# x and the first weights in eight shared transfers, compressed scores from whole queries, TensorE's steps in a new order

## The chip, the cores and the metric

One Trainium2 chip, one core. The engines are TensorE (PE, with its weight loads PEld), VectorE (DVE), ScalarE (ACT), GpSimd (POOL) and SyncE (SP), which only issues transfers here. The metric is the device time of one execution in microseconds, the median of several; the kernel before has 271.18 (three runs, 270.7 to 273.65).

## What is computed

Two decoder layers over x of 256 positions by 1024 channels, float32. The even layer has one input projection that feeds two groups of heads, NSA (8 heads; compressed blocks, selected blocks and a window, with gates) and MoBA (8 heads), each with its own gating path; the odd layer is gated linear attention (GLA, 4 heads). Each layer ends in a LayerNorm.

```python
def even_layer(x, w_in, ..., w_out, ln_g, ln_b):
    h = x @ w_in
    nq, nkv, ngate, nz, mq, mk, mv, mz = _split(h, EVEN_SPLITS)
    ...
    y = jnp.concatenate([o_nsa * jax.nn.silu(nz), o_moba * jax.nn.silu(mz)], axis=-1) @ w_out
    return layer_norm(DEEPNORM_ALPHA * x + y, ln_g, ln_b)

def odd_layer(x, w_in, gate_w2, gate_b, gn_g, w_out, ln_g, ln_b):
    h = x @ w_in
    q, k, v, g_lr, z = _split(h, ODD_SPLITS)
    log_a = jax.nn.log_sigmoid((g_lr @ gate_w2 + gate_b).astype(f32)) / GLA_TAU
    o = gla_mix(q, k, v, log_a)
    ...
    y = (o * jax.nn.silu(z)) @ w_out
    return layer_norm(DEEPNORM_ALPHA * x + y, ln_g, ln_b)
```

The compressed branch of NSA scores each query against 15 compressed keys; these scores are what the step s computes.

## The kernel before

**Products.** A dense product is done with both operands split in two: hi is the operand rounded to TensorE's 32-bit format (a cast), lo the rest (a subtraction). Each product is three matmuls, hi by hi, hi by lo, lo by hi. The contraction over 1024 channels is eight blocks of 128; `denseB` gives a result of 128 columns of the weights by 256 positions (24 matmuls), `denseA` one of 128 positions by up to 512 columns (24 matmuls).

**Weights.** They come in units of 1024 to 1120 columns of 128 partitions, in the order of the steps. `load_unit` issues the unit's transfer on SP into one of six raw buffers (`wr`); a transfer waits until the unit six earlier has been split. `split_unit` casts hi on ACT and subtracts lo on DVE or POOL, as the string `LO_ON` says by unit (V or G), into one of eight slots. `prepare_for` keeps the splits about two units ahead of the step that uses them.

**The head.** The first two units (K and V columns that the compressed branch needs, called "first") come in four halves of 256 KB on SP, x transposed (xT) in four pieces of 256 KB on ACT's queue. Each of four rounds casts one weight half and one xT piece on ACT and makes the low halves on DVE; TensorE does 12 matmuls a round into two PSUM banks (48 in all, one line in the profile, L324). Seven idle matmuls run before. Then Q0.0 and Q0.1, the first queries, are two `denseB` steps of their own on the next two units.

**The order.** TensorE's and SP's orders are the order in which the code is written, given by the step strings `EVEN` and `ODD`. Q, C, V, k, q, v, z, e, o with a number are dense steps; w, h, g, s, t, u are the compressed branch of NSA; Nja to Nje the scores, transposes and outputs of the NSA head group j (a and b scores, c, d transposes of the exponentials, e outputs), Mja, Mjc, Mje those of MoBA; in the odd layer n and N are LayerNorm, T the transposes of its rows, G and g the gate, I and L the levels of GLA, X its diagonals, A its outputs, U the gated rows. ACT, DVE and POOL run in an order fixed by a scheduler when the kernel is built; each engine does its instructions strictly in that order, so a late one holds what stands behind it. `AT_ODD` says behind which step a small load (gate weights, masks, LayerNorm weights) is issued.

**Attention steps.** For a head, DVE computes masked scores and their maxima, ACT the exponentials, and then the rows are scaled by 1/sum (times the gate for NSA) on the engine that `SC_ON` names for that step (A, V or G). TensorE transposes the scaled rows into one of two t banks, ACT copies them to SBUF (PT), and the outputs follow. PSUM has three d banks, two s, two t and one o.

**Names used.** hilo is a split unit, raw an unsplit one, pr the exponentials, PT their transposes, xt the split x, gl the transposed gate input, gw the gate's weights (gwh, gwl its halves), zg the gated rows. The function `cmp_s` is the step s: per head group t it multiplies the compressed keys kcf with the hi and then with the lo part of the queries, 4 matmuls each.

Of the kernel before, what the change touches and what calls it, by code (L numbers as in the profile page):

```python
# [7 lines left out]
F32 = mybir.dt.float32  # L8
# [7 lines left out]
P = 128  # L16
# [11 lines left out]
EVEN = """Q0.0 Q0.1 C0.0 V0.0 N0a C0.1 V0.1 w Q1.0 N0b h v0.0 N1a g Q1.1 v0.1 s N0c N1b N0d t k0.0 N1c k0.1 N2a u q0.0  # L28
N2b N1d N0e M0a q0.1 N2c N1e N2d M1a M0c k1.0 N3a N2e N3b M1c k1.1 q1.0 q1.1 z0.0 M0e M2a N3c z1.0 N3d M3a
M1e z0.1 M2c N3e M3c z2.0 z2.1 M2e z1.1 M3e z3.0 z3.1"""  # L30
# [4 lines left out]
ODD = """e0.0 e1.0 e0.1 n0 T0 e1.1 v1.0 v3.0 v0.0 n1 T1 v3.1 v0.1 G k0.1 g k0.0 q0.0 q0.1 q1.1 k1.1 I0 L1:0 k1.0 q1.0  # L35
L2:0 L4:0 v1.1 L8:0 I1 v2.0 L1:1 z0.0 z0.0+ L2:1 L4:1 z0.1 L8:1 z0.1+ L16:1 L16:0 z1.0 L32 z1.1 z1.0+ L64
v2.1 X L128 A0 z1.1+ U0 A1 o0.0 U1 o1.0 N0 o1.1 o0.1 N1"""
AT_EVEN = {"Q0.1": "w1", "N1c": "ln ev", "z3.0": "x"}
AT_ODD = {"k0.1": "gate", "e0.0": "masks", "q1.1": "ln od"}

LO_ON = "VVVVGGVVVVVGVVVVVGVVVVGVVVGVGVVVGGGGVVVVVGVVVGVGVGVVVVVVVVVVVVVVVVGVGVVV"

CP_ON = "AAVV"

SC_ON = "AVAGAGAVVVGV"
MK_BUFS = 2
# [67 lines left out]
def build(tc, I, out):  # L114
# [12 lines left out]
    with ExitStack() as ctx:  # L127
# [32 lines left out]
        def load_unit():  # L160
            k, n = SHAPES[len(raws)]
            raw = wr.tile([P, UMAX], F32, tag="raw", name=nm("raw"))
            rv = raw[:, :k * n].rearrange("p (k n) -> p k n", k=k)
            src = I["w"][at[0]:at[0] + P * k * n].rearrange("(p k n) -> p k n", p=P, k=k)
            at[0] += P * k * n
            for ks in ((slice(0, 2), slice(2, 4)) if len(raws) < 2 else (slice(0, k),)):
                nc.sync.dma_start(rv[:, ks], src[:, ks])
            raws.append(rv)

        def split_unit():  # L170
            u = len(units)
            k, n = SHAPES[u]
            t = wx.tile([P, 2, UMAX], F32R, tag="hilo", name=nm("hilo"))
            hv = t[:, :, :k * n].rearrange("p a (k n) -> p a k n", k=k)
            units.append(hv)
            if u < 2:
                return
            A.copy(hv[:, 0], raws[u])  # L178
            ENG[LO_ON[u]].tensor_sub(hv[:, 1], raws[u], hv[:, 0].bitcast(F32))  # L179

# [62 lines left out]

        xq = [cp.tile([P, 4, S], F32, tag=f"x{h}", name=nm("xT")) for h in range(2)]
        load_unit()
        for q in range(4):
            A.dma_start(xq[q // 2][:, 2 * (q % 2):2 * (q % 2) + 2], I["xT"][:, 2 * q:2 * q + 2])
        load_unit()
# [56 lines left out]

        xt = new_xt()
        fill[0] = 7
        pks = [bank("d"), bank("d")]
        prepare(2)
        for q in range(4):  # L310
            xs = xq[q // 2][:, 2 * (q % 2):2 * (q % 2) + 2]
            ks = slice(2 * q, 2 * q + 2)
            hv, rv = units[q // 2], raws[q // 2]
            us = slice(2 * (q % 2), 2 * (q % 2) + 2)
            A.copy(hv[:, 0, us], rv[:, us])
            A.copy(xt[:, 0, ks], xs)  # L316
            V.tensor_sub(hv[:, 1, us], rv[:, us], hv[:, 0, us].bitcast(F32))
            V.tensor_sub(xt[:, 1, ks], xs, xt[:, 0, ks].bitcast(F32))
            for n in range(3):
                for k in range(2 * q, 2 * q + 2):  # L320
                    for i in range(2):
                        wh, wl = (t[:, i * P:(i + 1) * P] for t in tile_of("first", k))
                        a, b = ((wh, xt[:, 0, k]), (wl, xt[:, 0, k]), (wh, xt[:, 1, k]))[n]
                        T.matmul(pks[i][:, :S], a, b, start=(k == n == 0), stop=(k == KC - 1 and n == 2))  # L324
        prepare(4)
# [17 lines left out]
        for i, pd in enumerate(pks):  # L343
            split_psum(KH[:, i], KL[:, i], pd[:, :S])
# [21 lines left out]
        def queries(j, i):  # L366
            pd = bank("d")
            denseB(pd[:, :S], f"even Q{j}", i, xt)
            q = [ep.tile([P, S], F32R, name=f"Q{n}{2 * j + i}") for n in "hl"]
            split_psum(*q, pd[:, :S])  # L370
            Q.append(q)
# [638 lines left out]
def layout(inputs):  # L1010
# [45 lines left out]
```

## Time and profile before

| | |
|---|---|
| median of three runs | 271.18 us |
| lowest, highest | 270.7, 273.65 us |
| the profiled execution, by its own time | 271.48 us |
| its span in the profile | 269.7 us |
| TensorE busy | 258.1 us, 96% |
| DVE, ACT, POOL busy | 188.7, 163.7, 69.4 us |
| TensorE's dense steps, L221 and L202 | 112.1 and 90.2 us busy |

The rows that follow are of one profiled execution. Times count from the start of its span. An engine is busy while it has an instruction under way; matmuls are pipelined, so the spans of neighbouring ones overlap. "Idle before" in square brackets is what the engine stood still just before a group, with what released it.

### The profile page before, as it was taken

To read this page: it belongs to the slowest core of one execution; us is meant where nothing else is said; L and a number is where in the kernel's file an instruction comes from. 1 tells how busy PE (TensorE), PEld (TensorE's weight loads), DVE (VectorE), ACT (ScalarE), POOL (GpSimd) and SP (SyncE) were. 2 spreads that over 40 slices of the span, in tenths; PEclk is the share of its full clock that TensorE was granted. 3 is DMA by queue.
4 is the path that set the end of the run, shared out by engine and by line. 5 is a ranking of instruction groups with operands and counts; after the bars stand their busy time and mean duration, and the time that the engine had idled before them with its cause. 6 is when DMAs were issued, how large, how long until landed. Compare 5 with 4: busy or idle time off the path is not lost.

```text
span 269.7 us, 5534 instructions
## 1 busy us (share of the span) xinstructions
PE 258.1 (96%) x2111; PEld 226.6 (84%) x2111; DVE 188.7 (70%) x411; ACT 163.7 (61%) x383; POOL 69.4 (26%) x58
## 2 busy tenths in 40 slices
PE   5999999999999999999999999999999999899990
PEld 2999987879887999899888899899997779688880
DVE  2888699796675575648839994657793793675745
ACT  4776658879887857845407526696973746853000
POOL 1070030823500344039402350807000003510101
PEclk9999999999999999999999999999999999999997
DMA  6999968754431062005950664775374260000012
GB/s 201 416 378 407 408 228 251 266 193 198 156 91 70 2 202 113 0 2 187 370 237 21 220 233 169 239 306 179 139 239 154 84 229 2 1 2 0 12 66 78
DMA packets 15035, 45.50 MB, mean 169 GB/s; under 512 B 2673, under 2 KB 3825, under 8 KB 15009
## 3 DMA queue, kind: packets, MB, share of 16 engines
q1 hardware_dynamic: 13856, 43.59, 45.4%
q10 hardware_dynamic: 1152, 1.57, 1.8%
q8 instruction: 16, 0.26, 0.4%
q14 instruction: 11, 0.08, 0.1%
HBM read 44.10 MB, written 1.05 MB: 167 GB/s over the span
## 4 chain that ended last, share of the span: by engine, by line
PE 80%; DVE 9%; DMA 3%; issue 3%; ACT 2%; POOL 1%; DVEq 0%; SPq 0%; ACTq 0%; POOLq 0%
PE d L202 31%; PE d L221 29%; PE s L338 3%; PE d L324 3%; DVE hilo L179 3%; PE t L549 2%; DVE x L288 2%; DMA gw<-gw 2%; ACT hilo L178 1%; DMA raw<-w 1%; PE o L569 1%; PE o L612 1%; PE t L603 1%; DVE x L290 1%; DVE lnst L276 1%
## 5 line engine op out<-in xcount | busy, mean ns | idle before, releaser
L221 PE MATMUL d<-hilo,xt 128*128 128x512 f32 (+3 forms) x600 | 112.1, 344 | 0.2 <-DVE xt L154 0.2
L221 PEld LDWEIGHTS d<-hilo,xt 128*128 128x128 f32 x600 | 93.4, 188 | 14.1 <-DVE xt L154 0.4
L202 PE MATMUL d<-xt,hilo 128*128 128x256 f32 x720 | 90.2, 284 | 0.0
L202 PEld LDWEIGHTS d<-xt,hilo 128*128 128x128 f32 x720 | 86.9, 189 | 1.3 <-issue 1.1
L178 ACT CAST hilo<-raw 128x1024 fp32r<-128x1024 f32 (+2 forms) x68 | 71.0, 1053 | 18.6 <-PE d L221 13.9
L179 DVE TENSOR_TENSOR hilo<-raw,hilo 128x1024 fp32r<-128x1024 f32 (+2 forms) x51 | 70.6, 1391 | 14.5 <-ACT hilo L178 14.3
L179 POOL TENSOR_TENSOR hilo<-raw,hilo 128x1024 fp32r<-128x1024 f32 (+1 forms) x17 | 44.5, 2627 | 125.5 <-ACT hilo L178 113.1
L496 ACT ACTIVATE pr<-ng,sm 128x256 f32<-128x256 f32 (+1 forms) x48 | 21.3, 445 | 7.7 <-DVE sm L495 7.7
L502 POOL TENSOR_SCALAR pr<-pr,sm 128x256 f32<-128x256 f32 (+1 forms) x12 | 11.8, 1000 | 19.3 <-DVE sm L532 13.4
L495 DVE CUSTOM_DVE_ANT_0 ng<-s,b 128x256 f32<-128x256 f32 (+1 forms) x48 | 14.2, 351 | 1.4 <-PE s L338 1.2
L275 DVE SCALAR_TENSOR_TENSOR x<-x,d 128x512 f32<-128x512 f32 (+1 forms) x9 | 5.6, 626 | 12.8 <-PE d L221 12.5
L256 POOL TENSOR_TENSOR lnrs<-lnrs,nhalf 128x1 f32<-128x1 f32 x4 | 2.9, 731 | 33.3 <-DVE lnrs L255 33.3
L324 PEld LDWEIGHTS d<-xt,hilo 128*128 128x128 f32 x48 | 7.7, 249 | 2.4 <-ACT xt L316 2.4
L324 PE MATMUL d<-xt,hilo 128*128 128x256 f32 x48 | 7.9, 339 | 1.5 <-ACT xt L316 1.5
L496 ACT ACTIVATION_READ_ACCUMULATOR pr<-ng,sm 128x1 f32 x48 | 9.0, 188 | 0.0
L636 DVE TENSOR_TENSOR xt<-g,xt 128x256 fp32r<-128x256 f32 x8 | 6.7, 833 | 2.8 <-ACT xt L635 2.8
L288 DVE SCALAR_TENSOR_TENSOR x<-x,lnmv,lng 128x256 f32<-128x256 f32 x16 | 8.5, 592 | 0.0
L976 ACT ACTIVATE xt<-t,gnh 128x128 fp32r<-128x128 f32 x16 | 4.3, 383 | 6.1 <-PE t L973 6.1
L635 ACT CAST xt<-g 128x256 fp32r<-128x256 f32 x8 | 3.3, 407 | 7.8 <-DVE g L634 7.6
L552 ACT COPY PT<-t 128x512 f32<-128x512 f32 (+1 forms) x16 | 7.2, 474 | 1.0 <-PE t L549 0.9
L502 DVE TENSOR_SCALAR pr<-pr,sm 128x256 f32<-128x256 f32 (+1 forms) x20 | 7.5, 435 | 0.2
L795 POOL TENSOR_TENSOR TT<-TT 128x512 f32<-128x512 f32 (+5 forms) x6 | 5.0, 827 | 8.9 <-ACT TT L792 8.5
(191 smaller groups left out, 269.6 us busy)
## 6 DMA issues: line engine op xcount, KB each, us to landing
raw<-w SPq DMA_DIRECT2D x58, 512.0 KB, 4.7
raw<-w SPq DMA_DIRECT2D x8, 520.0 KB, 7.0
w<-w SPq DMA_DIRECT2D x4, 512.0 KB, 8.2
raw<-w SPq DMA_DIRECT2D x2, 560.0 KB, 7.2
xT<-xT ACTq DMA_DIRECT2D x4, 256.0 KB, 6.1
raw<-w SPq DMA_DIRECT2D x4, 256.0 KB, 5.6
x<-x SPq DMA_DIRECT2D x2, 512.0 KB, 3.7
b<-b SPq DMA_DIRECT2D x1, 512.0 KB, 7.5
```

Source lines behind the costliest of these rows:

```text
L178: A.copy(hv[:, 0], raws[u])
L179: ENG[LO_ON[u]].tensor_sub(hv[:, 1], raws[u], hv[:, 0].bitcast(F32))
L202: T.matmul(o, a, b, start=(j == 0), stop=(j == len(terms) - 1))
L221: T.matmul(o, a, b, start=(ks[0] == j == 0), stop=(ks[-1] == KC - 1 and j == len(terms) - 1))
L288: V.scalar_tensor_tensor(x[:, sl], x[:, sl], mv[:, 0:1], g[:, sl], ALU.subtract, ALU.mult)
L324: T.matmul(pks[i][:, :S], a, b, start=(k == n == 0), stop=(k == KC - 1 and n == 2))
L338: T.matmul(o, a[halves[g]], b[halves[g]], start=(n == 0), stop=(n == len(terms) - 1))
L495: V.tensor_tensor_reduce(ng[:, :w], pS, b8[:, h, S - w:], -0.125, 3e38, ALU.add, ALU.min, sm[:, 0:1])
L496: A.activation(pr, ng[:, :w], AF.Exp, bias=sm[:, 0:1], scale=-1.0, accum_out=sm[:, 1:2])
L502: ENG[e].tensor_scalar(pr, pr, coef, None, ALU.mult)
L552: A.copy(dst, pt[:, :2 * P * (c + 1)].rearrange("p (a q) -> p a q", q=P))
L636: V.tensor_sub(mx[:, 1, k], g2, mx[:, 0, k].bitcast(F32))
```

## The change

Three edits.

1. **The head.** The two units of "first" and the two of Q0 are no longer units of the weight stream. Block k of xT (256 columns) and block k of both sets of weights (512 columns) come together in one transfer of 128 by 768 (393 KB), eight in all, on SP, into the six raw buffers, so block 6 and block 7 wait until blocks 0 and 1 have been split. The 96 matmuls (those of "first" and of Q0) run block by block into four banks (two d, two s). The cast of xT is on DVE for the first two blocks, on ACT for the rest. Q0 has no separate matmuls; its queries and KH, KL are split at the end of the head.
2. **s from whole queries.** ACT also copies each query tile whole (128 by 256), and `cmp_s` multiplies kcf with these, 4 matmuls instead of 8.
3. **Orders and engines.** The strings EVEN, ODD, AT_ODD, `LO_ON` (20 splits on POOL instead of 17), `CP_ON` and `SC_ON` (which engine scales each step's rows) are new.

The diff, cut to its core:

```diff
-EVEN = """Q0.0 Q0.1 C0.0 V0.0 N0a C0.1 V0.1 w Q1.0 N0b h v0.0 N1a g Q1.1 v0.1 s N0c N1b N0d t k0.0 N1c k0.1 N2a u q0.0
-N2b N1d N0e M0a q0.1 N2c N1e N2d M1a M0c k1.0 N3a N2e N3b M1c k1.1 q1.0 q1.1 z0.0 M0e M2a N3c z1.0 N3d M3a
-M1e z0.1 M2c N3e M3c z2.0 z2.1 M2e z1.1 M3e z3.0 z3.1"""
-ODD = """e0.0 e1.0 e0.1 n0 T0 e1.1 v1.0 v3.0 v0.0 n1 T1 v3.1 v0.1 G k0.1 g k0.0 q0.0 q0.1 q1.1 k1.1 I0 L1:0 k1.0 q1.0
-L2:0 L4:0 v1.1 L8:0 I1 v2.0 L1:1 z0.0 z0.0+ L2:1 L4:1 z0.1 L8:1 z0.1+ L16:1 L16:0 z1.0 L32 z1.1 z1.0+ L64
-v2.1 X L128 A0 z1.1+ U0 A1 o0.0 U1 o1.0 N0 o1.1 o0.1 N1"""
+EVEN = """Q0.0 Q0.1 C0.0 C0.1 N0a V0.0 V0.1 w Q1.0 N0b h v0.0 N1a g Q1.1 v0.1 s N1b N0d k0.0 t N2a N1c q0.0 N0c k0.1 u
+N2b N1d N0e M0a q0.1 N2c N1e M0c M1a k1.0 N2d N3a N2e N3b k1.1 M1c q1.0 z0.0 M0e M2a N3c M1e z1.0 q1.1 N3d
+z0.1 M2c N3e M3a M2e z2.0 z2.1 M3c z1.1 M3e z3.0 z3.1"""
+ODD = """e0.0 e1.0 e0.1 n0 T0 e1.1 v3.0 v1.0 n1 v0.0 T1 v3.1 v0.1 G k0.1 k0.0 g k1.1 q0.0 q1.1 q0.1 v1.1 I0 L1:0 k1.0
+q1.0 L2:0 L4:0 v2.0 I1 L8:0 z0.0 L1:1 z0.0+ L2:1 L4:1 z0.1 L8:1 L16:0 z0.1+ v2.1 z1.0 L16:1 L32 z1.1 L64
+z1.0+ X A0 L128 z1.1+ U0 A1 o0.0 U1 o1.0 o1.1 N0 o0.1 N1"""
 AT_EVEN = {"Q0.1": "w1", "N1c": "ln ev", "z3.0": "x"}
-AT_ODD = {"k0.1": "gate", "e0.0": "masks", "q1.1": "ln od"}
-LO_ON = "VVVVGGVVVVVGVVVVVGVVVVGVVVGVGVVVGGGGVVVVVGVVVGVGVGVVVVVVVVVVVVVVVVGVGVVV"
-CP_ON = "AAVV"
-SC_ON = "AVAGAGAVVVGV"
+AT_ODD = {"v3.1": "gate", "v3.0": "masks", "L1:0": "ln od"}
+LO_ON = "VVVGGVVGVVVVVGGVVVVVVVGVVGVGGVVVGGGGVGVVVVVVVVGGVGVGVVVVVVVVVVGVVGVVGVVV"
+CP_ON = "AVAV"
+SC_ON = "GVGAGAAGAAAV"
...
+            if len(raws) < 4:
+                raws.append(None)
+                return
             raw = wr.tile([P, UMAX], F32, tag="raw", name=nm("raw"))
             rv = raw[:, :k * n].rearrange("p (k n) -> p k n", k=k)
-            src = I["w"][at[0]:at[0] + P * k * n].rearrange("(p k n) -> p k n", p=P, k=k)
+            nc.sync.dma_start(rv, I["w"][at[0]:at[0] + P * k * n].rearrange("(p k n) -> p k n", p=P, k=k))
             at[0] += P * k * n
-            for ks in ((slice(0, 2), slice(2, 4)) if len(raws) < 2 else (slice(0, k),)):
-                nc.sync.dma_start(rv[:, ks], src[:, ks])
             raws.append(rv)
...
+            k, n = SHAPES[u] if u >= 4 else (2, 512)
             t = wx.tile([P, 2, UMAX], F32R, tag="hilo", name=nm("hilo"))
             hv = t[:, :, :k * n].rearrange("p a (k n) -> p a k n", k=k)
             units.append(hv)
-            if u < 2:
+            if u < 4:
                 return
...
-        xq = [cp.tile([P, 4, S], F32, tag=f"x{h}", name=nm("xT")) for h in range(2)]
-        load_unit()
-        for q in range(4):
-            A.dma_start(xq[q // 2][:, 2 * (q % 2):2 * (q % 2) + 2], I["xT"][:, 2 * q:2 * q + 2])
-        load_unit()
+        heads = []
+        for k in range(KC):
+            raw = wr.tile([P, UMAX], F32, tag="raw", name=nm("raw"))[:, :S + 512]
+            nc.sync.dma_start(raw, I["head"][k])
+            heads.append(raw)
...
-        fill[0] = 7
-        pks = [bank("d"), bank("d")]
-        prepare(2)
-        for q in range(4):
-            xs = xq[q // 2][:, 2 * (q % 2):2 * (q % 2) + 2]
-            ks = slice(2 * q, 2 * q + 2)
-            hv, rv = units[q // 2], raws[q // 2]
-            us = slice(2 * (q % 2), 2 * (q % 2) + 2)
-            A.copy(hv[:, 0, us], rv[:, us])
-            A.copy(xt[:, 0, ks], xs)
-            V.tensor_sub(hv[:, 1, us], rv[:, us], hv[:, 0, us].bitcast(F32))
-            V.tensor_sub(xt[:, 1, ks], xs, xt[:, 0, ks].bitcast(F32))
+        fill[0] = WARM
+        pks = [bank(t) for t in "ddss"]
+        prepare(4)
+        for k, raw in enumerate(heads):
+            hi, lo = units[k // 2][:, 0, k % 2], units[k // 2][:, 1, k % 2]
+            A.copy(hi, raw[:, S:])
+            copied_by("V" if k < 2 else "A", xt[:, 0, k], raw[:, :S])
+            V.tensor_sub(xt[:, 1, k], raw[:, :S], xt[:, 0, k].bitcast(F32))
+            V.tensor_sub(lo, raw[:, S:], hi.bitcast(F32))
             for n in range(3):
-                for k in range(2 * q, 2 * q + 2):
-                    for i in range(2):
-                        wh, wl = (t[:, i * P:(i + 1) * P] for t in tile_of("first", k))
-                        a, b = ((wh, xt[:, 0, k]), (wl, xt[:, 0, k]), (wh, xt[:, 1, k]))[n]
-                        T.matmul(pks[i][:, :S], a, b, start=(k == n == 0), stop=(k == KC - 1 and n == 2))
-        prepare(4)
+                for i in range(4):
+                    a, b = ((hi, xt[:, 0, k]), (hi, xt[:, 1, k]), (lo, xt[:, 0, k]))[n]
+                    T.matmul(pks[i][:, :S], a[:, i * P:(i + 1) * P], b, start=(k == n == 0), stop=(k == KC - 1 and n == 2))
...
-        for i, pd in enumerate(pks):
+        for i, pd in enumerate(pks[:2]):
...
-            pd = bank("d")
-            denseB(pd[:, :S], f"even Q{j}", i, xt)
+            pd = bank("d") if j else pks[2 + i]
+            if j:
+                denseB(pd[:, :S], f"even Q{j}", i, xt)
             q = [ep.tile([P, S], F32R, name=f"Q{n}{2 * j + i}") for n in "hl"]
             split_psum(*q, pd[:, :S])
-            Q.append(q)
+            whole = ep.tile([P, S], F32, tag="osb", bufs=8, name=f"Q{2 * j + i}")
+            A.copy(whole, pd[:, :S])
+            Q.append(q + [whole])
...
-            for n in range(2):
-                for t in range(4):
-                    T.matmul(psT[32 * t:32 * t + 32, :S], cmp["kcf"].rearrange("p g n -> p (g n)"),
-                             Q[t][n].bitcast(F32), start=(n == 0), stop=(n == 1), tile_position=(0, 32 * t))
+            for t in range(4):
+                T.matmul(psT[32 * t:32 * t + 32, :S], cmp["kcf"].rearrange("p g n -> p (g n)"), Q[t][2],
+                         start=True, stop=True, tile_position=(0, 32 * t))
...
-    a["xT"] = np.ascontiguousarray(inputs["x"][0].T.reshape(KC, P, S).transpose(1, 0, 2))
-    units = []
-    for (source, cs, rows), n in zip(TILES.values(), UNITS.values()):
-        w = inputs[source][0][np.array(rows)][:, np.array(cs)].reshape(n, KC // n, P, len(cs))
+    units, heads = [], [inputs["x"][0].T]
+    for (name, (source, cs, rows)), n in zip(TILES.items(), UNITS.values()):
+        w = inputs[source][0][np.array(rows)][:, np.array(cs)]
+        if name in HEAD:
+            heads.append(w)
+            continue
+        w = w.reshape(n, KC // n, P, len(cs))
         units += [w[i].transpose(1, 0, 2).ravel() for i in range(n)]
     a["w"] = np.concatenate(units)
+    a["head"] = np.ascontiguousarray(np.concatenate(heads, 1)).reshape(KC, P, -1)
```

What moves, at the three places that the prediction speaks of:

ACT around the scaled rows of M0 (pr of the first MoBA step). Before, behind the four exponentials of M0 (the L496 with 128x256 among them) the casts and the mq cast and N2c's two PT copies follow.

```order
L496 ACTIVATE pr_1028,sm_1027<-ng_1030,sm_1027 128x128
L496 ACTIVATE pr_1028,sm_1027<-ng_1033,sm_1027 128x256
L496 ACTIVATE pr_1029,sm_1027<-ng_1036,sm_1027 128x128
L496 ACTIVATE pr_1029,sm_1027<-ng_1039,sm_1027 128x256
L178 CAST hilo_1352<-raw_1042 128x1024
L153 CAST mq_935<-d_1047 128x256
L178 CAST hilo_1384<-raw_1161 128x1024
L552 COPY PT_1085<-t_1087 128x512
L552 COPY PT_1086<-t_1093 128x512
```

After, M0's four scalings (L500) stand among them.

```order
L496 ACTIVATE pr_1044,sm_1043<-ng_1046,sm_1043 128x128
L496 ACTIVATE pr_1044,sm_1043<-ng_1049,sm_1043 128x256
L496 ACTIVATE pr_1045,sm_1043<-ng_1052,sm_1043 128x128
L496 ACTIVATE pr_1045,sm_1043<-ng_1055,sm_1043 128x256
L182 CAST hilo_1368<-raw_1058 128x1024
L500 ACTIVATE pr_1044<-pr_1044,sm_1043 128x128
L156 CAST mq_905<-d_1063 128x256
L500 ACTIVATE pr_1044<-pr_1044,sm_1043 128x256
L500 ACTIVATE pr_1045<-pr_1045,sm_1043 128x128
L500 ACTIVATE pr_1045<-pr_1045,sm_1043 128x256
L552 COPY PT_1101<-t_1103 128x512
L552 COPY PT_1102<-t_1109 128x512
```

Before, these scalings were DVE's; N2c's PT copies (the L552 of 128x512) now stand behind them, and M0c's transposes need the two t banks that these copies release.

DVE before and behind the transposes T1 of the second LayerNorm of the even layer (x_1805 and x_1821 are its rows, xt its split transposes). Before:

```order
L179 TENSOR_TENSOR hilo_2130<-raw_2029,hilo_2130 128x1024
L283 BN_AGGR lnmv_2164<-lnst_1856 128x2
L255 TENSOR_SCALAR lnrs_2165<-lnmv_2164 128x1
L288 SCALAR_TENSOR_TENSOR x_1805<-x_1805,lnmv_2164,lng_864 128x256 x4
L290 SCALAR_TENSOR_TENSOR x_1805<-x_1805,lnrs_2165,lnb_866 128x256 x4
L154 TENSOR_TENSOR xt_1854<-t_2177,xt_1854 128x4x128
L154 TENSOR_TENSOR xt_1854<-t_2184,xt_1854 128x4x128
L726 TENSOR_TENSOR gwl<-gw,gwh 48x512
```

After:

```order
L183 TENSOR_TENSOR hilo_2159<-raw_2043,hilo_2159 128x1024
L260 TENSOR_SCALAR lnrs_2145<-lnmv_2144 128x1
L293 SCALAR_TENSOR_TENSOR x_1821<-x_1821,lnmv_2144,lng_891 128x256 x4
L295 SCALAR_TENSOR_TENSOR x_1821<-x_1821,lnrs_2145,lnb_893 128x256 x4
L183 TENSOR_TENSOR hilo_2164<-raw_2048,hilo_2164 128x1024
L726 TENSOR_TENSOR gwl<-gw,gwh 48x512
L157 TENSOR_TENSOR xt_1870<-t_2193,xt_1870 128x4x128
L157 TENSOR_TENSOR xt_1870<-t_2200,xt_1870 128x4x128
```

A split (hilo_2164) and the gate's gwl now stand between the LayerNorm and the low halves of xt.

TensorE at the end of GLA: X (L909), L128 (L888), A0 (L944), z1.1+ (L221 or L225), U0 (L973). Before:

```order
L909 MATMUL t_3012<-ident,attL 128x128 x4
L888 MATMUL s_3026<-KQ 128x128 x4
L944 MATMUL o_3032<-VV,att_1869 128x256 x2
L944 MATMUL s_3033<-VV,att_1869 128x256 x2
L221 MATMUL d_2946<-hilo_2892,xt_1854 128x512 x6
L221 MATMUL d_2946<-hilo_2897,xt_1854 128x512 x6
L973 MATMUL t_3076<-ident,zg 128x128 x4
```

After:

```order
L909 MATMUL t_3038<-ident,attL 128x128 x4
L944 MATMUL o_3052<-VV,att_1885 128x256 x2
L944 MATMUL s_3053<-VV,att_1885 128x256 x2
L888 MATMUL s_3068<-KQ 128x128 x4
L225 MATMUL d_2998<-hilo_2920,xt_1870 128x512 x6
L225 MATMUL d_2998<-hilo_2925,xt_1870 128x512 x6
L973 MATMUL t_3092<-ident,zg 128x128 x4
```

L128 now stands behind A0, and z1.0+ (not shown) just ahead of X in place of v2.1.

## Rows read from the trace of the kernel before

**Rows 1.** Page, part 1: engine, busy us (share of the span), instructions
```profile
PE 258.1 (96%) x2111; PEld 226.6 (84%) x2111; DVE 188.7 (70%) x411; ACT 163.7 (61%) x383; POOL 69.4 (26%) x58
```

**Rows 2.** Waits of TensorE: engine, line, waited for: us in total, times, longest
```profile
PE t L973 <- DVE zg L960: 0.7, 1, 0.7
...
PE s L202 <- DVE gl L772: 0.5, 1, 0.5
...
PE t L466 <- ACT PT L552: 0.2, 1, 0.2
...
PE d L221 <- DVE xt L154: 0.2, 1, 0.2
```

**Rows 3.** Timeline of the start: start us, us, engine, line, operation, out<-in, count
```profile
4.70 0.62 ACT L315 CAST hilo<-raw 128x512 fp32r<-128x512 f32 x1 [0.58 <-DMA raw<-w]
...
5.88 7.88 PE L324 MATMUL d<-xt,hilo 128*128 128x256 f32 x48 [1.53 <-ACT xt L316]
...
13.60 6.60 PE L202 MATMUL d<-xt,hilo 128*128 128x256 f32 x54
```

**Rows 4.** Busy time by stretch: us, PE PEld DVE ACT POOL, PEclk, DMA share, GB/s
```profile
2.00:4.40 2.40, 2.35 (x6) 0.60 (x4) 0.00 (x0) 1.49 (x2) 0.00 (x0) 1.00 0.85 237
...
5.88:10.10 4.22, 4.21 (x19) 4.22 (x20) 3.72 (x7) 3.36 (x6) 0.00 (x0) 1.00 1.02 398
10.10:19.31 9.21, 9.21 (x78) 9.21 (x78) 7.74 (x9) 7.32 (x10) 4.77 (x2) 1.00 1.06 392
```

**Rows 5.** Timeline, compressed scores (L458) and the next step (L549)
```profile
53.87 0.64 PE L458 MATMUL t<-Qh,kcf 128*32 128x256 f32 x8
...
54.87 1.30 PE L549 MATMUL t<-ident,pr 128*128 128x128 f32 x8
```

**Rows 6.** Timeline, DVE before the gate's products
```profile
171.79 0.41 DVE L772 TENSOR_TENSOR gl<-t,gl 16x256 fp32r<-16x256 f32 x1
```

**Rows 7.** Timeline, the end of GLA: L128, z1.1+ and the gated rows
```profile
227.66 1.06 PE L888 MATMUL s<-KQ 128*128 128x128 f32 x8
...
230.10 3.15 PE L221 MATMUL d<-hilo,xt 128*128 128x512 f32 x12
...
233.39 0.88 DVE L960 SCALAR_TENSOR_TENSOR zg<-o,rs,zg 128x256 f32<-128x256 f32 x2 [1.13 <-POOL rs L256]
```

**Rows 8.** Timeline, around M0's scaled rows, ACT and DVE, and N2d on TensorE
```profile
72.19 1.28 ACT L500 ACTIVATE pr<-pr,sm 128x128 f32<-128x128 f32 x4
...
75.13 1.03 ACT L178 CAST hilo<-raw 128x1024 fp32r<-128x1024 f32 x1
...
75.47 1.01 DVE L502 TENSOR_SCALAR pr<-pr,sm 128x128 f32<-128x128 f32 x4
...
76.07 0.36 ACT L153 CAST mq<-d 128x256 fp32r<-128x256 f32 x1
...
77.28 1.05 ACT L552 COPY PT<-t 128x512 f32<-128x512 f32 x2
...
78.29 0.66 PE L549 MATMUL t<-ident,pr 128*128 128x128 f32 x4
```

**Rows 9.** Timeline, DVE before and behind T1
```profile
156.63 3.50 DVE L288 SCALAR_TENSOR_TENSOR x<-x,lnmv,lng 128x256 f32<-128x256 f32 x4
...
160.06 1.66 DVE L290 SCALAR_TENSOR_TENSOR x<-x,lnrs,lnb 128x256 f32<-128x256 f32 x4
...
162.16 1.40 DVE L154 TENSOR_TENSOR xt<-t,xt 128x512 fp32r<-128x512 f32 x2 [0.45 <-ACT xt L153]
```

**Rows 10.** The gate's weights: transfer to landing, and the subtraction
```profile
L726 DVE TENSOR_TENSOR gwl<-gw,gwh x1: 685/685/685, 166.1 to 166.1; 48x512 fp32r<-48x512 f32 x1
...
DMA to landing us min/median/max: 5.4/5.4/5.4
```

**Rows 11.** Timeline, DVE: a split that met a POOL split, and the next
```profile
17.15 3.21 DVE L179 TENSOR_TENSOR hilo<-raw,hilo 128x1120 fp32r<-128x1120 f32 x1 [0.31 <-ACT hilo L178]
...
20.68 1.31 DVE L179 TENSOR_TENSOR hilo<-raw,hilo 128x1120 fp32r<-128x1120 f32 x1
```

More of the change, by code (lines that the diff above doesn't have):

```diff
@@ L48 @@
 FILL = 6
+WARM = 7
+HEAD = ("first", "even Q0")
 WX = 8
@@ L171, in split_unit @@
             u = len(units)
-            k, n = SHAPES[u]
+            k, n = SHAPES[u] if u >= 4 else (2, 512)
             t = wx.tile([P, 2, UMAX], F32R, tag="hilo", name=nm("hilo"))
@@ L514, in nsa_scores @@
             pS = [bank("s")[:, :2 * w].rearrange("p (b k) -> p b k", b=2) for g in range(2)]
-            qh, ql = (q[:, c * P:(c + 1) * P] for q in Q[t])
+            qh, ql = (q[:, c * P:(c + 1) * P] for q in Q[t][:2])
             kh, kl = (k[:, :, :w] for k in (KH, KL))
```

## The prediction

> **What bounds the kernel now.** I read the page first, then the waits of TensorE, then stretches of the timeline around each wait and around the steps that the change moves. TensorE is busy for 258.1 us, 96% of the span [rows 1]; whatever does not shorten its line of steps, or its waits, is not seen in the time. Its waits inside the program are few [rows 2]: 0.7, 0.5, 0.2 and 0.2 us; the rest of its idle time is the start, before the first product, and the last LayerNorm, which the change leaves as it is. So the other engines only matter where they would make TensorE wait, and a new order can win about 1.5 us inside the program plus what the head gives. It can lose more than that, since each of the moved steps may open a new wait.
>
> **Gain 1, the head.** Before, the first product starts at 5.88, after a weight piece (cast from 4.70, 0.62 us) and an xT piece that was cast behind it on ACT and for which TensorE waited 1.5 us; the 48 products of the first tile end where the next tile's begin, at 13.60, and the 48 of Q0 follow [rows 3]. Until 10.1 us TensorE issues 19 products of 256 columns in 4.22 us, behind it 78 in 9.21 [rows 4]: about 0.213 us each, which is 256 columns at 1.2 GHz, and then 0.119, the level of 2.4 GHz with what lies between products. The granted-clock column reads 1.00 in both, so I take the level from the pace. With 48 x 0.119 = 5.7 us for Q0, C0.0 starts at 13.60 + 5.7 = 19.3.
>
> After, block 0 is one transfer of 393 KB on SP's queue, and its two hi casts lie side by side (weights on ACT, x on DVE). Between 2.0 and 4.4 us the DMA moved 237 GB/s [rows 4], 0.57 MB, enough for one block; I place its landing at 4.3, between 3.7 (0.393 MB by that rate) and 4.7 (the first piece now). With a cast of 0.62 the first product starts at about 4.95. All 96 products then run back to back: four banks give twelve products per block, 2.56 us at the slow pace and 1.43 at the fast one, while a block takes about 1 us to arrive at 410 GB/s and about 1 us on ACT (0.62 and some 0.36) and on DVE, so data is never late, also for blocks 6 and 7, whose buffers come free only when blocks 0 and 1 are split. With a clock rise at time R the 96th ends at R + (96 - (R - 4.95)/0.213) x 0.119. If the clock rises 4.2 us after the first product as now, R is 9.15 and C0.0 starts at 18.2 (1.1 earlier); if at 10.1 as now, 18.6 (0.7 earlier); if at 8.4, 17.9 (1.4); if at 11.8, 19.4 (0). I take 0.9, with 0 to 1.4 for the range. The half-speed products cost the same number of microseconds whichever they are; the gain is only the earlier start and rise. Moving xT off ACT's queue frees ACT of four issues, but gives no bandwidth. The Trainium skill ("Trainium Kernel Development and Optimization", Key Constraints) says the same: the engines' DMA queues share one set of DMA engines.
>
> **Gain 2, compressed scores.** s takes from 53.87 to 54.87 now, 16 records [rows 5]; half of them go: 0.5. The four copies of whole queries (some 0.36 us each on ACT) lie under C0 and Q1, where nothing on TensorE waits for them at once.
>
> **Gain 3, waits that go.** t waited 0.2 for a PT copy; k0.0 (24 products at 0.119, 2.9 us) now stands ahead of t: 0.2. g waited 0.5 for gl, whose DVE part started only at 171.79, behind a split on DVE [rows 2, 6]; k0.0 now stands ahead of g as well, another 2.9 us of cover: 0.5. U0 waited 0.7 for the gated rows, ready on DVE at about 233.9, while the only cover was z1.1+ from 230.10 [rows 2, 7]; L128, whose eight records span 1.06 us (0.9 without the pipelined end), moves between A0 and z1.1+, so the cover is longer by 0.9: 0.7 is won. L128's own copy on ACT is behind the squares in the order of after, so they start as soon as before. Sum 1.4; with the head 0.9 and s 0.5: **2.8**.
>
> **Loss 1, M0c.** M0c stood behind N2d, which began at 78.29, and M1a; it now comes straight behind N1e, so at 78.29 on the time line of before. What must be ready is M0's scaled rows. DVE did them in 1.01 us from 75.47. After, they are on ACT, in its fixed order: four exponentials, then a 1024-column cast (1.03, row at 75.13), one scaling, the mq cast, three scalings, and only then the two PT copies of N2c (1.05 us), whose t banks M0c needs. ACT did four scalings of 128 in 1.28 us [rows 8], 0.32 each, and I estimate 0.42 for 256 columns: 75.13 + 1.03 + 0.36 + 2 x 0.32 + 2 x 0.42 + 1.05 = 79.05, against 78.29 wanted: 0.75. DVE's subtraction ahead of the exponentials can also be held by a POOL split running then. I take 0.9, with 0 to 1.3.
>
> **Loss 2, T1 to v3.1.** DVE ended LayerNorm at 160.06 + 1.66 = 161.72 and began the low half of xt at 162.16, for which v3.1 waited 0.2 already [rows 2, 9]. After, DVE has one more split (some 1.2) and gwl (0.7) ahead of it, 1.9 us; two splits that POOL did there are now DVE's, but without POOL the LayerNorm's first four operations are no longer slowed (3.5 us before, some 1.7 after). Net the low half starts at about 163.0 to 163.8: 0.8 more wait. The gate's transfer is issued two units earlier, but its cast now stands ahead of the xt casts in ACT's order; it took 5.4 us to land [rows 10], and if it does so again from about 157, the xt casts are held until some 163: 1.8. I take 0.8, with 0 to 1.8.
>
> **Loss 3, the other moved steps.** N1c directly behind t and N2a waits for DVE's scaling (0 to 0.5), N0c for a PT copy (0 to 0.15), N2e for N2d's PT behind M1's scalings on ACT (0 to 0.6), h for the folded part behind a split (0 to 0.2). Each is bounded by one PT copy of 0.53 or two scalings; most have a dense step of 2.9 us ahead that hides them. 0.3 together, 0 to 1.4.
>
> **POOL's added work** (three splits, four more scalings) costs nothing by itself: POOL is busy 26% of the span. But DVE pays: a split that met POOL's took 3.21 us on DVE [rows 11] where the next of the same size took 1.31, so 1.9 is lost each time, until POOL's instruction ends. The Trainium skill ("SBUF — State Buffer", "SBUF: two separate sides") states this as an exclusive lock of a shared port pair for the whole instruction, against a DVE operation with two SBUF inputs; by that rule the change pays for its moves, and the trace agrees where the two met. Where a hold falls on a DVE operation that TensorE waits for, it appears as a wait at that step; the taken sums hold one such (at M0c).
>
> **The sum.** 271.48 (the profiled execution; 269.7 of span and 1.8 around it) - 2.8 + 0.9 + 0.8 + 0.3 = 270.7. That execution lies 0.3 above the median of 271.18, so 270.4 for a median.
>
> **Rivals.**
> - *The waits stay hidden* (chance 0.28). ACT and DVE arrive in time at M0c and v3.1, and the clock rises early in the denser head. Then 271.2 - 1.4 - 1.9 is 267.9, and 268.4 with 0.5 of the losses. For it: DVE and ACT are idle for 30 and 39% of the span; LayerNorm sheds its slow operations. Against it: the orders of both engines are fixed, and the casts stand ahead at just these places.
> - *ACT becomes the bound of the attention steps* (0.11, slower). It scales 10 times 128 and 14 times 256 columns instead of 16 times 128: 9.1 us instead of 5.1, and 1.4 for whole queries. If M0c, N2e, M1c and their followers each wait for ACT, up to 4.0 more lands on TensorE: 270.4 + 4.0 - 0.9 is 273.5. It decides once waits exceed the gains of 2.8 by 2.7, 5.5 in all. Against it: dense steps of 2.9 us between attention steps let ACT catch up.
> - *POOL holds DVE* (0.08). Seven more POOL operations, 1.9 each at most, are 13 us on DVE, which is idle for 30% of the span, 81 us. If one in ten of these microseconds reaches TensorE beyond the sum, it is 271.7; at one in four, 273.7.
> - *The head changes nothing* (0.08). Block 0 lands at 4.7 or later, the clock rises later, C0.0 starts at 19.3: 271.3.
>
> **Chances.** The forecast has 0.45, its own range 269.3 to 271.8. About 1% (2.7 us) is what a measurement of this kernel can tell from no change. Faster by more than that is the first rival and a little of the forecast's edge: 0.29; slower is the second and part of the third: 0.13; within 1%: 0.58. The range is 267.7 to 272.9, from the first rival to most of the way to the second.
>
> **What would show it.** In the profile of after: first head product at 4.95 and C0.0 at 18.2 to 18.7; 8 records in the compressed scores; no wait before g, t and U0; a wait of some 0.9 before M0c's transposes and of about 1 at v3.1. If M0c and v3.1 show none, losses 1 and 2 were my errors, and the time is below 269. If TensorE idles at many of the attention steps on ACT, the second rival holds.

## The result and the profile after

The changed kernel takes 267.19 us (median of four, 267.08 to 267.55) against 272.36 for before in the same comparison; the ratio is 0.984, with an interval of 0.980 to 0.988. It is faster by 1.2 to 2.0%. The forecast of 270.4 was too high, and 267.19 lies 0.5 below its range (as a ratio to 271.18 the range began at 0.987, just inside the measured interval); the first rival (the waits stay hidden, 267.9) came closest. The profiled execution took 267.55, with a span of 265.8.

TensorE's waits in after, which answer to [rows 2] and to the 1.5 us of [rows 3] (engine, line, what it waited for, us in total, times, longest; the row that names DVE idle is the memset ahead of the warm-up, as in before):

```profile
PE d L225 <- ACT xt L156: 1.4, 1, 1.4
PE d L147 <- DVE idle L245: 1.2, 1, 1.2
PE d L225 <- DVE xt L157: 0.2, 1, 0.2
```

The waits before t, g and U0 are gone, none came before M0c, and one of 1.4 us stands in front of v3.1 (L225 is `denseA`, L221 in before). The points at which TensorE reaches a stage, in its timeline (the first two rows are the warm-up and the first products):

```profile
1.19 3.17 PE L147 MATMUL d<-idle 128*128 128x512 bf16 x7 [1.19 <-DVE idle L245]
4.51 0.79 PE L323 MATMUL d<-xt,hilo 128*128 128x256 f32 x2
...
16.93 5.99 PE L206 MATMUL d<-xt,hilo 128*128 128x256 f32 x48
...
125.80 9.41 PE L225 MATMUL d<-hilo,xt 128*128 128x512 f32 x40
...
157.53 1.04 PE L713 MATMUL t<-ident,x 128*128 128x128 f32 x8
...
166.29 0.38 PE L770 MATMUL t<-ident,VV 128*16 128x128 f32 x2
...
230.00 1.27 PE L973 MATMUL t<-ident,zg 128*128 128x128 f32 x8
...
241.26 17.11 PE L225 MATMUL d<-hilo,xt 128*128 128x512 f32 x96
```

From 16.93 on these are C0.0, the first step of the odd layer, T1, G, U0 and the last products. With the same points of before:

| stretch | reached at its end, before | after | gained | forecast |
|---|---|---|---|---|
| to C0.0 | 19.31 | 16.93 | 2.38 | 0.9 |
| C0.0 to the odd layer | 129.15 | 125.80 | 0.97 | -0.5 (s and t, less M0c and the other steps) |
| to T1 | 160.91 | 157.53 | 0.03 | 0 |
| T1 to G | 168.52 | 166.29 | -1.15 | -0.8 |
| G to U0 | 233.93 | 230.00 | 1.70 | 1.2 (g, U0) |
| to the last product's end | 262.49 | 258.38 | 0.18 | 0 |
| behind it (span less that) | 7.21 | 7.38 | -0.17 | 0 |

The sum is 3.94, against 0.8 forecast. Three terms were off: the head (2.4 for 0.9), M0c with the other moved steps (nothing for 1.2), and the wait at v3.1 (1.15 for 0.8). They make 2.3 of the 3.1 us between the two sums. The rest, 0.3 ahead of the odd layer and 0.5 between G and U0, is not traced: no idle time of TensorE in either kernel accounts for it.

### The profile page after: what moved, and what is told of

Its sections match the earlier page's. It is cut to its first block, busy times and chain, and to the rows that moved or that the text cites. A ratio compares the mean times of both kernels' runs of the same rounds, so it can differ in the third digit from the quotient of the medians.

```text
span 265.8 us, 5536 instructions
## 1 busy us (share of the span) xinstructions
PE 255.4 (96%) x2103; PEld 225.3 (85%) x2103; DVE 174.3 (66%) x404; ACT 167.5 (63%) x399; POOL 75.1 (28%) x65
## 4 chain that ended last, share of the span: by engine, by line
PE 87%; DVE 6%; DMA 3%; issue 2%; ACT 1%; DVEq 0%; SPq 0%
PE d L225 34%; PE d L206 31%; PE s L336 3%; PE d L323 3%; PE t L549 2%; PE s L323 2%; DMA gw<-gw 2%; DVE hilo L183 2%; PE o L569 1%; PE o L612 1%; DMA raw<-head 1%; PE t L603 1%; DVE x L293 1%; DVE x L295 1%; DVE lnst L281 1%
## 5 line engine op out<-in xcount | busy, mean ns | idle before, releaser
L225 PE MATMUL d<-hilo,xt 128*128 128x512 f32 (+3 forms) x600 | 111.8, 344 | 1.6 <-ACT xt L156 1.4
L225 PEld LDWEIGHTS d<-hilo,xt 128*128 128x128 f32 x600 | 93.1, 188 | 15.7 <-ACT xt L156 1.6
L206 PE MATMUL d<-xt,hilo 128*128 128x256 f32 x672 | 84.6, 284 | 0.0
L206 PEld LDWEIGHTS d<-xt,hilo 128*128 128x128 f32 x672 | 81.2, 189 | 1.2 <-issue 0.7
L183 POOL TENSOR_TENSOR hilo<-raw,hilo 128x1024 fp32r<-128x1024 f32 (+1 forms) x20 | 50.1, 2515 | 100.5 <-ACT hilo L182 89.7
L183 DVE TENSOR_TENSOR hilo<-raw,hilo 128x1024 fp32r<-128x1024 f32 (+2 forms) x46 | 60.5, 1324 | 22.8 <-ACT hilo L182 22.6
L496 ACT ACTIVATE pr<-ng,sm 128x256 f32<-128x256 f32 (+1 forms) x48 | 21.4, 449 | 6.3 <-DVE sm L495 6.2
L502 POOL TENSOR_SCALAR pr<-pr,sm 128x128 f32<-128x128 f32 (+1 forms) x16 | 12.5, 798 | 20.7 <-PE t L549 11.9
L323 PE MATMUL d<-xt,hilo 128*128 128x256 f32 x48 | 10.3, 297 | 0.2
L323 PE MATMUL s<-xt,hilo 128*128 128x256 f32 x48 | 9.9, 288 | 0.0
L500 ACT ACTIVATE pr<-pr,sm 128x256 f32<-128x256 f32 (+1 forms) x24 | 9.5, 456 | 0.2 <-DVE sm L589 0.2
L496 ACT ACTIVATION_READ_ACCUMULATOR pr<-ng,sm 128x1 f32 x48 | 9.1, 190 | 0.0
L323 PEld LDWEIGHTS d<-xt,hilo 128*128 128x128 f32 x48 | 7.8, 201 | 1.3 <-ACT hilo L316 1.1
L552 ACT COPY PT<-t 128x256 f32<-128x256 f32 (+1 forms) x16 | 7.0, 472 | 1.3 <-PE t L549 1.3
L323 PEld LDWEIGHTS s<-xt,hilo 128*128 128x128 f32 x48 | 7.7, 198 | 0.0
L633 DVE SCALAR_TENSOR_TENSOR g<-th,d 128x256 f32<-128x256 f32 x8 | 3.4, 420 | 6.5 <-ACT th L632 6.2
```

Source lines behind the costliest of these rows:

```text
L206: T.matmul(o, a, b, start=(j == 0), stop=(j == len(terms) - 1))
L225: T.matmul(o, a, b, start=(ks[0] == j == 0), stop=(ks[-1] == KC - 1 and j == len(terms) - 1))
L323: T.matmul(pks[i][:, :S], a[:, i * P:(i + 1) * P], b, start=(k == n == 0), stop=(k == KC - 1 and n == 2))
L496: A.activation(pr, ng[:, :w], AF.Exp, bias=sm[:, 0:1], scale=-1.0, accum_out=sm[:, 1:2])
L500: A.activation(pr, pr, AF.Copy, scale=coef)
L502: ENG[e].tensor_scalar(pr, pr, coef, None, ALU.mult)
```

## The experiments

Each was timed against before; times are medians.

**A gap behind the warm-up.** In after the first product follows the seven idle matmuls at 0.15 us (4.36 to 4.51); in before 1.5 us lay between. With four of them the gap is back (1.28 us).

```diff
-WARM = 7
+WARM = 4
```

> After with 4 idle warm-up matmuls in place of 7, so TensorE stands still from about 3.0 us to the first product at 4.5, as long as in before. Theory clock (the fast pace comes early in after because no gap lies between warm-up and products): the fast pace starts at 8.7 to 10.1 us instead of 6.0, about 20 to 26 products run at 0.21 us, C0.0 starts at 17.8 to 18.6 instead of 16.93, and the time is 268.2 to 268.9 against 267.2. Rival (four banks and block-by-block order alone make the head fast): the pace rises near 6 as in after, C0.0 at 16.9, time 267.2.

C0.0 at 18.51, time 267.99 (267.28 to 268.34). TensorE's products from 6 to 8 us (columns as in [rows 4]), of after and then of this kernel:

```profile
6.00:8.00 2.00, 2.00 (x19) 2.00 (x19) 0.78 (x2) 0.93 (x2) 0.00 (x0) 1.00 0.99 379
```

```profile
6.00:8.00 2.00, 2.00 (x12) 2.00 (x11) 0.52 (x2) 0.67 (x2) 0.00 (x0) 1.00 1.01 387
```

19 products against 12 (some of the 12 overlap the edges; the pace was 0.21 us each until about 10). The clock theory's numbers came, 1.6 us at C0.0; the time rose only by 0.8, because the wait at v3.1 fell from 1.4 to 1.0 and so gave part of it back. Four matmuls are also less work ahead of the first product, 1.89 us instead of 3.17, so this run does not part the gap from the shorter warm-up.

**Before with a longer warm-up.** The gap closed in before, nothing else.

```diff
-        fill[0] = 7
+        fill[0] = 11
```

> Before with 11 warm-up matmuls in place of 7, so that they reach to the first product (about 6.1 us). Theory clock: the fast pace starts near 6 us, the 48 products of the head end with the last piece's casts at about 11.9 instead of 13.60, C0.0 starts at about 17.6 instead of 19.31, and the time is 1.6 below before: 269.6. Rival (gap of no account): the pace rises at 10.1 or later, C0.0 at 19.3 to 19.6, time as before or 0.3 above.

The head's products now ran fast from the start and ended at 11.86 instead of 13.60, but TensorE then waited 0.65 for a DVE split, and the odd layer began only 0.85 earlier. The time is unchanged: 271.29, ratio 0.999 (0.995 to 1.002). The profiled execution took 274.21, 2.9 above that median, so it need not show where the others lost the lead. In this one the rest was lost at the gate: 0.72 us of wait at G, 1.82 at g, and then the clock fell (columns as in [rows 4]):

```profile
172.00:176.00 4.00, 2.38 (x14) 2.25 (x15) 2.51 (x4) 1.82 (x4) 3.33 (x2) 0.88 0.75 230
176.00:180.00 4.00, 4.00 (x26) 4.00 (x26) 1.53 (x2) 3.02 (x4) 0.00 (x0) 0.70 0.74 214
```

```profile
168.66 0.28 PE L770 MATMUL t<-ident,VV 128*16 128x128 f32 x1 [0.72 <-ACT VV L761]
...
173.62 0.38 PE L202 MATMUL s<-gl,gwh 48*128 48x256 f32 x1 [1.82 <-DVE gl L772]
```

```profile
176.00:180.00 4.00, 4.00 (x36) 4.00 (x35) 2.63 (x3) 3.97 (x6) 0.00 (x0) 1.00 0.74 298
```

A granted clock of 0.88 and 0.70, 26 products in 4 us where before, in the last line, did 36 at 1.00: the 120 products behind g took 16.07 us instead of 14.56. The wait at g and what followed it took 3.3 us.

**The gate's load back behind k0.1, in after.**

```diff
-AT_ODD = {"v3.1": "gate", "v3.0": "masks", "L1:0": "ln od"}
+AT_ODD = {"k0.1": "gate", "v3.0": "masks", "L1:0": "ln od"}
```

> After with the gate's weights loaded behind k0.1 as in before, so that their cast stands behind the xt casts on ACT. Theory gate (the 1.4 us in front of v3.1 is the transfer of the gate's weights): that wait falls to 0.1 to 0.5 in all, the time to 266.1. Rival (DVE's extra split ahead of xt is what is late): a wait of 1 us or more stays in front of v3.1, named DVE, and the time stays within 0.4 of 267.2.

266.60, between the two expectations; 0.24 and 0.22 of wait at v3.1, G reached 1.17 earlier than in after. So the wait was the transfer, with the cast that waits for it. In after it reads (SP's issue, ACT's casts, TensorE):

```profile
153.08 0.42 SPq L722 DMA_DIRECT2D gw<-gw  x1
...
158.54 0.62 ACT L725 CAST gwh<-gw 48x512 fp32r<-48x512 f32 x1 [3.31 <-DMA gw<-gw]
...
159.33 1.06 ACT L156 CAST xt<-t 128x512 fp32r<-128x512 f32 x2
...
159.96 0.51 PE L225 MATMUL d<-hilo,xt 128*128 128x260 f32 x2 [1.39 <-ACT xt L156]
```

The transposes T1 had ended at 158.6, but ACT stood at gwh until the weights landed, and the cast of xt stood behind it.

**After's head and scores in before's orders and tables.** (The strings EVEN to SC_ON of before in after's kernel.)

> After's head and compressed scores with before's orders and engine tables. If the parts add up: C0.0 at 16.9 (2.4 earlier than before), s half as long (0.5), the waits of 0.2, 0.5 and 0.7 us before t, g and U0 back, T1 to v3.1 with 0.2; time 271.2 - 2.9 = 268.3. If the gains of the head are lost again in an order that was made for the old one: new waits in the even layer and 269.5 or more.

271.68, ratio 0.998 (0.994 to 1.002): nothing is left. C0.0 was reached at 17.24, 2.1 earlier than in before. TensorE then waited 0.65 for a split that before's table gives to POOL, 0.26 and 0.25 in the compressed branch, and the lead at T1 was 0.96. The rest went at g:

```profile
19.78 1.46 PE L206 MATMUL d<-xt,hilo 128*128 128x256 f32 x10 [0.65 <-POOL hilo L183]
...
165.36 0.62 ACT L725 CAST gwh<-gw 48x512 fp32r<-48x512 f32 x1 [3.50 <-DMA gw<-gw]
...
171.75 0.41 DVE L772 TENSOR_TENSOR gl<-t,gl 16x256 fp32r<-16x256 f32 x1
...
172.22 0.38 PE L206 MATMUL s<-gl,gwh 48*128 48x256 f32 x1 [1.44 <-DVE gl L772]
```

The weights landed at 165.4 as in before, gl came at 171.8 as in [rows 6], and TensorE, a microsecond earlier, waited a microsecond longer. gwh holds ACT, ACT's later casts hold DVE, and gl is at their end. The split just ahead of gl took 2.59 us on DVE beside a split on POOL, where one ahead of it took 1.23, so it is part of the chain too.

**The gate's load at e0.0, in before, in the mixed kernel and in after.** It is issued some 30 us earlier there (in after at 123.1 instead of 153.1).

```diff
-AT_ODD = {"k0.1": "gate", "e0.0": "masks", "q1.1": "ln od"}
+AT_ODD = {"e0.0": "gate", "v3.0": "masks", "q1.1": "ln od"}
```

> Before with the gate's weights loaded at e0.0 (lands some 30 us before they are needed; the masks move to v3.0). Theory landing (the 0.5 us at g in before, and its slower executions of 273 to 276, come from the late landing of the gate's weights, which holds ACT's casts and then gl on DVE): no wait at g, median 270.6 to 271.0, hardly an execution above 272.5. Rival (the wait at g comes from DVE's split held by POOL): the wait stays at 0.4 to 0.6, and the spread of before stays.

> After's head and scores with before's orders, and the gate's weights loaded at e0.0. Theory landing (what the new head won was given back at g, because the weights landed at 165.4 us whatever TensorE's lead was): no wait at g, the lead of 0.97 us at G stays to the end, median 269.7 to 270.3. Rival (the split on DVE holds gl): a wait of 1 us or more stays at g and the time is 271.2 or more.

> After with the gate's weights loaded at e0.0. Theory landing: in front of v3.1 only 0.2 to 0.5 us of wait in all instead of 1.6; also gwl no longer stands between the LayerNorm and xt on DVE; no new wait at g; median 265.8 to 266.3. Rival (DVE's other split ahead of xt is late as well): 0.8 us or more stay, 266.5 or more.

The load does not land sooner after its issue. In after it was issued behind six transfers of 512 KB and took 9.1 us, and ACT stood 1.86 us for it; but no instruction that TensorE needed soon stood behind it:

```profile
123.11 0.39 SPq L722 DMA_DIRECT2D gw<-gw  x1
...
132.25 0.62 ACT L725 CAST gwh<-gw 48x512 fp32r<-48x512 f32 x1 [1.86 <-DMA gw<-gw]
```

Before falls to 270.20, ratio 0.994 (0.992 to 0.997); its eight times lie between 269.99 and 270.47, those of before beside them between 270.42 and 273.55. The wait at g is gone in both old orders, though in before the split ahead of gl still took 2.35 us beside POOL: without the late landing it has slack. The mixed kernel takes 269.94, after with the early load 266.62 (265.99 to 267.15), its span 0.9 below after's; what is left at v3.1 is:

```profile
PE d L225 <- ACT xt L156: 0.2, 1, 0.2
PE d L225 <- DVE xt L157: 0.2, 1, 0.2
```

266.6 is the lowest time of the study, reached with either place of the load. Against after it is 0.6 lower in the median, which the two intervals (0.977 to 0.984, and 0.980 to 0.988) do not separate; in the traces T1 to G is 1.16 us shorter with the early load, of which 0.24 had been lost ahead of T1.

**Before's head and scores with after's tables, late and early load.**

> Before's head and compressed scores with after's orders and engine tables. C0.0 at 19.3 as in before. If the tables' part is what I worked out: no waits at t, g and U0 (1.4 gained), 0.9 to 1.4 in front of v3.1, so 270.2 to 270.7. If the new tables need the new head (units split on POOL early, Q0 steps in front): new waits before w and 271 or more.

> Before's head and scores with after's orders and tables, the gate's weights loaded at e0.0: the fourth corner beside before's (270.2) and after's (266.6) and the mixed kernel with after's head in before's orders (269.9), all three without a wait for the gate's weights. If head and tables add up, the tables alone are worth as much here as on after's head, 3.3: 266.9. If they need each other: 268.3 to 269.5, with waits for splits before w (0.8, 0.6 and 0.3 were seen there in the same kernel with the late gate).

270.92 with the late load, between its two expectations; new waits of 0.63, 0.78 and 0.33 came ahead of w. Its profiled execution took 272.98, with 1.7 us of wait at v3.1. With the early load 269.71 (269.51 to 269.85), more than either expectation. So the four corners without a wait for the gate's weights are:

| | before's tables | after's tables |
|---|---|---|
| before's head and scores | 270.20 | 269.71 |
| after's head and scores | 269.94 | 266.62 |

The head and scores alone bring 0.3, the tables alone 0.5, both together 3.6. With the old tables the new head's lead of 1.20 at C0.0 (17.64 against 18.84) is down to 0.36 by v0.0, and 0.59 are left at the odd layer, although s is shorter; the waits seen are 0.29 for a split on POOL and 0.25 for the transposes behind s, the rest is in shorter pieces. With the new tables the old head reaches C0.0 at 19.76, 2.37 later than the new one, then waits 0.3 for DVE, and s takes 0.43 more: the odd layer begins 3.37 later (129.38 against 126.01), and the gap stays about that size to the end. So there the head's lead is kept whole.

**One NSA step's scalings on ACT again.** They stood ahead of M0's exponentials on ACT in before, the 1.28 us in [rows 8].

```diff
-SC_ON = "GVGAGAAGAAAV"
+SC_ON = "GVGAAAAGAAAV"
```

> After with one NSA step's scalings (the ones that before did on ACT ahead of M0's exponentials) on ACT again instead of POOL: 4 times 0.32 us more on ACT there. If my loss at M0c failed because these scalings had left ACT: a wait of 0.4 to 0.7 us appears in front of M0c's transposes, and the time is 267.5 to 267.9. If ACT had slack there in any case: no wait at M0c, 267.2.

In after ACT began the cast ahead of M0's scalings at 71.37, and M0c did not wait:

```profile
71.37 1.03 ACT L182 CAST hilo<-raw 128x1024 fp32r<-128x1024 f32 x1
...
73.97 1.04 ACT L552 COPY PT<-t 128x512 f32<-128x512 f32 x2
...
74.91 0.88 PE L603 MATMUL t<-ident,pr 128*128 128x128 f32 x6
```

With the scalings back:

```profile
72.25 1.03 ACT L182 CAST hilo<-raw 128x1024 fp32r<-128x1024 f32 x1
...
74.85 1.04 ACT L552 COPY PT<-t 128x512 f32<-128x512 f32 x2
...
75.47 1.03 PE L603 MATMUL t<-ident,pr 128*128 128x128 f32 x6 [0.47 <-ACT PT L552]
```

ACT is 0.88 later from here on and M0c waits 0.47, as expected. The times (268.08, from 266.78 to 269.85) spread too much to show 0.5; the trace shows it.

**The compressed scores from halves again, in after.** (`cmp_s` and the copies as in before.)

> After with the compressed scores from hi and lo as in before: 8 matmuls instead of 4, and without the four whole-query copies on ACT. 0.5 us more at s; 0.4 to 0.6 more in all (267.6 to 267.8) if nothing behind it absorbs it; about 0.1 to 0.3 if the wait in front of v3.1 shrinks by a part of it.

269.04, 1.85 more than after: more than either expectation. In after s reads, with the step behind it:

```profile
51.59 0.64 PE L458 MATMUL t<-Q,kcf 128*32 128x256 f32 x8
52.16 0.39 PE L336 MATMUL s<-KH,Qh 64*128 64x256 f32 x2
```

and here:

```profile
51.85 0.64 PE L457 MATMUL t<-Qh,kcf 128*32 128x256 f32 x8
52.31 0.61 PE L457 MATMUL t<-Ql,kcf 128*32 128x256 f32 x8
52.85 0.39 PE L336 MATMUL s<-KH,Qh 64*128 64x256 f32 x2
```

1.00 instead of 0.57, so s itself is worth 0.43. The odd layer began at 126.34, 0.54 later, though C0.0 had come 0.19 earlier. Ahead of s the first scores, N0a, had lost 0.44: a split on POOL began at 19.92 instead of 20.71, a small DVE operation beside it took 2.56 us instead of 0.15, and the low half of the queries stands behind that on DVE:

```profile
19.92 2.81 POOL L183 TENSOR_TENSOR hilo<-raw,hilo 128x1120 fp32r<-128x1120 f32 x1 [2.96 <-ACT hilo L182]
...
20.20 2.56 DVE L349 TENSOR_SCALAR b1h<-cst 128x2 f32<-128x2 f32 x1
...
22.67 0.41 DVE L157 TENSOR_TENSOR Ql<-s,Qh 128x256 fp32r<-128x256 f32 x1
```

In front of v3.1 TensorE waited 1.34 us and 0.22, about as in after, but here the clock fell behind it (this kernel, then after):

```profile
158.00:166.00 8.00, 6.44 (x40) 6.00 (x39) 2.78 (x4) 3.23 (x7) 1.71 (x1) 0.79 0.26 91
```

```profile
158.00:166.00 8.00, 6.39 (x52) 5.94 (x51) 2.22 (x4) 5.17 (x8) 2.69 (x2) 1.00 0.27 87
```

After did 52 matmuls at 1.00 in this stretch, this kernel 40. T1 to G took 10.24 us instead of 8.76, and with the 0.54 that is what this execution (269.59) is longer by. It does not explain the median: three of the other five, with a mean granted clock of 0.993 or 0.994 as in after, took 268.15 to 269.40. What made those longer is open.

**The gap with the early load.** (After with the gate's load at e0.0 and `WARM = 4`.)

> After with the gate's weights loaded at e0.0 and 4 warm-up matmuls in place of 7, so TensorE stands still for about 1.3 us ahead of the first product; nothing behind the head can give the delay back at the gate. Theory clock: the fast pace starts at about 10 us as with 4 warm-ups before, C0.0 at 18.5 instead of 17.0 to 17.4, the time 1.1 to 1.5 above 266.6. If the gap does not decide it in each execution: C0.0 near 17.2 in the profiled one, and single times spread from 266.5 to 268.1.

267.25 (266.60 to 267.37), 0.6 above the early load with 7; C0.0 at 18.27 instead of 17.39. The fast pace came at about 9.5. This is less than the clock theory's 1.1 to 1.5: a late rise costs 0.9 at C0.0 in this pair.

## Why the forecast was wrong, step by step

- **The head, 0.9 for 2.4: the step that failed is the bounds of R.** The first product came at 4.51 (I had 4.95), worth 0.25 by my own line. The fast pace came at about 6.0, below my lowest bound of 8.4, because I counted from the first product and left out what TensorE had done before it; neither 8.4 nor 11.8 was read from a row. With a start of 4.51 and R = 6.0 the line gives 16.6, and a wait of some 0.2 us for a low half of x, which I had ruled out ("data is never late"), brings it to 16.8, near the 16.93 measured. The 2.4 holds against a late rise: in before with the early load, which rose near 6, C0.0 came at 18.84, 1.9 behind after. In all eight profiled kernels in which the gap behind the warm-up was 0.5 us or less, the pace rose by 7 us; in the six with a gap of 1.3 us or more it rose at 9.5 to 10.4 in four (before, both with 4 warm-ups, before's head with after's tables and the early load) and near 6 in two. Four of these six have before's head and seven matmuls of warm-up, as many as after, and two of the four rose late. So a late rise was seen only behind a gap, and the gap does not decide each execution; more than these fourteen executions there is not. The Trainium skill ("TensorE: Matmul & The Clock Gate", Part 1: The HAM clock gate) says that the same kernel starts its fast pace at differing points from run to run; the trace agrees, 6 and 10 us for the same head.
- **Scores, 0.5: right.** 8 records are left, and s takes 0.57 us, 0.43 less than with the others.
- **t, g, U0, 1.4: right in size, and for g half right in cause.** I put the wait at g down to DVE's split. That split is in the chain, but it was late by the landing of the gate's weights, two engines earlier; the run with the early load in before shows that the wait goes without the late landing. The price was right since k0.0 covers it in either case.
- **M0c, 0.9 for 0: the failing step is the start of ACT's chain at 75.13.** That row stood behind four scalings [rows 8] that the change itself moves to POOL (the fifth letter of SC_ON). Without those 0.9 us my 79.05 is 78.2, just under the 78.29 wanted. The run that put them back measured a wait at the place that I had forecast for after, 0.47 where I had 0.9.
- **T1 to v3.1, 0.8 for 1.15: right in place, near in size by luck.** I took DVE's extra work as the likelier cause and the landing as the bound of 1.8. It was the landing; DVE's low half came just 0.2 late, as in before.
- **The other moved steps, 0.3 for 0.** None shows a wait.
- **POOL and DVE: as forecast.** POOL is busy 75.1 us instead of 69.4 and DVE's splits beside it are stretched (one of 3.00 us at 166.14), but no wait of TensorE names them in after. In the mixed kernels a split on POOL did hold TensorE: by 0.65 with after's head in before's order, by 0.78 with before's head in after's order; and through DVE by 0.44 with the scores from halves.
- **The sum: parts that do not add.** I priced head and orders apart. The corners show that 2.8 of the 3.6 us come only with both: the head's lead was kept with the tables whose splits and loads are early enough for it, and mostly lost with the others. The first rival came closest since two of its conditions held, the early clock and M0c; the third, v3.1 in time, did not.

## What to carry to other kernels

Price a moved instruction on an in-order engine from what will stand ahead of it, with everything that the change itself takes off that engine ahead of it; a time read from a row of before is of use only after that. A gain at the start of a kernel is worth what the next late transfer leaves of it: look for the first wait that is tied to a landing, and move that load, or the cast that waits for it, to where nothing that TensorE needs soon stands behind it. Behind the xt casts and at e0.0 gave the same 266.6 here. Where a warm-up ends before the first product can start, lengthen it to meet it: worth 0.6 to 0.8 in after, and nothing in before, where what stood behind it could not follow.

## What the runs showed of the hardware that was not expected

- **A wait in the middle can cost about twice its length.** In single profiled executions, idle stretches of 1.39 and 0.22 us at v3.1 left the granted clock at 1.00 in after; 1.34 and 0.22 us brought it to 0.79 over eight microseconds in the kernel with the scores from halves, for 1.5 us more; 0.72 us at G and 1.82 at g brought it to 0.70, for 1.5 more; 1.72 and 0.22 us at v3.1 brought it to 0.50 over two microseconds in before's head with after's tables. A wait of 1.44 us at g (after's head in before's orders) did not. Removing the wait narrowed before's times from 270.4 to 273.6 down to 270.0 to 270.5.
- **A small transfer behind large ones lands like a large one.** The gate's weights, 48 rows of 512 words (96 KB), took 5.4 us to land in before and in after alike, where the 512 KB transfers of weight units took 4.7 in the median; 9.1 at e0.0 behind six of these, 3.5 in after with the load back behind k0.1, and 7.3 in the profiled execution of before with the longer warm-up (ACT's cast at 166.77, in before 165.40).
